# Hybrid decoder layer on one core: gate vectors as running sums, w_in splits moved ahead of the state scan, the attention sink as a 129th key, the gated unit by token tiles

## The chip, the cores and the metric

The kernel runs on one core of one Trainium2 chip. The metric is device time of one launch in microseconds (us), the median over runs. Five engines work side by side, each through its own queue of instructions in order: TensorE (PE, matmuls; its weight loads are listed as PEld), VectorE (DVE), ScalarE (ACT), GpSimd (POOL) and SyncE (SP), which here issues nearly all DMA transfers. Instructions of different engines are tied by semaphores. The order within each queue is fixed when the program is built.

## The reference

One decoder layer over x (1024 tokens by 1024), conditioned on one vector c:

```
mod = silu(c) @ w_ada + b_ada                       # sh1, sc1, g1, sh2, sc2, g2
h = rmsnorm(x, pre_mix_g) * (1 + sc1) + sh1
q, k, v, u = split(h @ w_in)                        # 512, 128, 128, 512 columns
attn = sliding_window_attention(q, k, v, sinks)     # 8 heads, 2 kv heads, window 128, ALiBi,
                                                    # softmax over the keys and one sink logit
ssm = s5_mixer(u, ...)                              # complex diagonal scan per group, then
                                                    # z = gelu(y); z * sigmoid(z @ w_glu + b_glu)
heads = concat(rmsnorm(attn), rmsnorm(ssm))
x = x + g1 * rmsnorm(heads @ w_out, post_mix_g)
h = rmsnorm(x, pre_mlp_g) * (1 + sc2) + sh2
x = x + g2 * rmsnorm(square(relu(h @ w_mlp_in)) @ w_mlp_out, post_mlp_g)
```

## The kernel before

Large products are done as three fp32r matmuls each (`mm3`, lines 85 to 87): high part by high part, high by low, low by high. So every operand is split first: ACT copies the high part, DVE (line 90, the helper `tt`) subtracts it to get the low part.

The order of the work is set by the tile scheduler: it simulates the program as written and gives every engine a fixed queue; tiles with the same tag share memory and so wait for one another (`slot("S3", ...)` is one place in SBUF, and a new tile there waits for the last reader of the old one). Only the PE queue of the MLP is written out by hand. The stages, with their lines and their place in the span:

- 0 to 113 us: loads, norm of x, the part of w_ada for sh1 and sc1, the u projection (`u_step`), and the small tables of the state space model. `mods2` (lines 460 to 480) adds up sh2 and sc2 on DVE as running sums over eight 128-row blocks of w_ada.
- 113 to 140 us: `vp`, the scan's inputs, and DVE's products that form `Vs`.
- 140 to 244 us: the q, k, v projections `pq` (lines 664 to 684), six passes m of 48 matmuls; each loads its columns into `wr`, and splits them into `whi` and `wlo`. Beside them the scan over 8 chunks on DVE (line 608), the tables `Gs` on POOL (lines 627 to 630), the products `kp` of them, their copy `K`, and eight DMAs (line 655) that spread K into the Toeplitz table `T`. `T` lies in the place of `S5`, whose last reader is the sum on K.
- 215 to 290 us: `yp` (lines 704 to 707), the state space output from T, Gs and Vs; gelu gives `z`, transposed and split to `zh`, `zl`.
- 252 to 376 us: attention in 16 units (`scores`, `probs_t`, `values`), with the softmax on DVE and ACT. Between the units lie the gated unit `glu(m, h)` (by blocks of 128 output features) and `gates()`, which computes g1 and g2 on PE in eight steps: 4 DMAs of w_ada into slot S3 (`graw`), 16 matmuls, a sum over partitions, a product with the gain on POOL, and a write to DRAM.
- 365 to 500 us: `po`, heads by w_out, in halves v=1 (ssm) and v=0 (attn); the weights come by `wor` into slots S0, S3, S1, S2 and are split into `woh` (ACT) and `wol` (DVE, two of them POOL). Then residual and second norm.
- 500 to 1202 us: the MLP, in a Strassen-like form, and the last norm.

Of the kernel before, what the change touches and what calls it, by code (L numbers as in the profile page):

```python
# [9 lines left out]
F32 = mybir.dt.float32  # L10
# [23 lines left out]
def tile_hymba(ctx: ExitStack, tc: tile.TileContext, x, c, w_ada, b_ada, pre_mix_g, w_in,  # L34
# [328 lines left out]
    def vecs2():  # L363
        small_loads()
        vps = ps("C", "vps")
        T.transpose(vps[:, 0:20], S5[0:20, 3840:3968], ident[0:20, 0:20])
        V.tensor_copy(vt[:, 64:84], vps[:, 0:20])
        V.tensor_scalar(bgl, bglu, 0.5, None, op0=MUL)
        V.tensor_scalar(nsk, snk, -1.0, None, op0=MUL)

    bgl = ct([P, 4], F32, "bgl")
    nsk = ct([P, 8], F32, "nsk")
# [86 lines left out]

    def mods2():  # L460

        for s in (3, 4):
            acc = slot("S7", [P, D], F32, "macc")
            for q in range(KC):
                ab = slot(("S3", "S6")[q % 2], [P, D], F32, "adm")
                pin(SY.dma_start(ab, w_ada_v[q, :, s * D:(s + 1) * D]))
                if q == 0:
                    pin(V.tensor_scalar(acc, ab, cact[:, 0:1], None, op0=MUL))
                else:
                    pin(V.scalar_tensor_tensor(acc, ab, cact[:, q:q + 1], acc, op0=MUL, op1=ADD))  # L470
                yield
# [10 lines left out]
    gd = {s: dp.tile([P, D], F32, name=f"gate{s}") for s in (2, 5)}  # L482
    w_ada_s = w_ada.rearrange("(q p) (s f) -> p q s f", p=P, s=6)

    def gates():

        gcols = slot("JK", [P, 2, 2 * P], F32, "gcols")
        for s in (2, 5):
            for b in range(4):
                sl = slice(2 * P * b, 2 * P * b + 2 * P)  # L490
                g = gcols[:, b % 2]
                SY.dma_start(g, (post_mix_g if s == 2 else post_mlp_g)[0, sl].partition_broadcast(P))
                srcs = []
                ap_ = ps("C", "ada")
                o = ap_[:, 2 * P:4 * P]
                raw = slot("S3", [P, 4, 2 * P], F32, "graw")
                for q in range(KC):
                    if q % 2 == 0:
                        SY.dma_start(raw[:, q % 4:q % 4 + 2], w_ada_s[:, q:q + 2, s, sl])
                    c0 = 32 * (q % 4)  # L500
                    T.matmul(ap_[c0:c0 + 32, 0:2 * P], cact32[:, q], raw[:, q % 4], start=q < 4, stop=q >= 4)
                part = parts_ada[:, b % 2]
                A.activation(part, ap_[:, 0:2 * P], AF.Copy)
                T.matmul(o, sel, part, start=True, stop=False)
                for e in range(2):
                    r = 64 + 8 * s + 2 * b + e
                    T.matmul(o[:, e * P:(e + 1) * P], ident[64:112, r:r + 1].broadcast_to([48, P]), vrow[64:112],
                             start=False, stop=e == 1)
                A.activation(part, o, AF.Copy)
                tt(PL, g, part, g, MUL)  # L510
                SY.dma_start(gd[s][:, sl], g)
                yield
# [83 lines left out]
    kk_ = ct([P, 2, G], F32, "kk")  # L596
    k1, k2 = kk_[:, 0], kk_[:, 1]
    for C in range(8):
        if C:

            y, x0 = Vs[:, C - 1, :, 15], Vs[:, C, :, 0]
            tt(V, k1, y, Bt[:, 0], MUL)
            tt(V, k2[0:64], y[64:128], Bt[64:128, 1], MUL)
            tt(V, k2[64:128], y[0:64], Bt[0:64, 1], MUL)
            tt(V, x0, x0, k1, ADD)
            tt(V, x0, x0, k2, ADD)
        blk = Vs[:, C].rearrange("p g d -> p (g d)")
        V.tensor_tensor_scan(blk, R, blk, 0.0, op0=MUL, op1=ADD)
# [12 lines left out]
    for qg in range(4):  # L621
# [27 lines left out]
    tt(PL, kd, bc(ident[0:CI, 0:CI], 1, G), bc(dsT, 2, CI), MUL)  # L649
    tt(PL, Kt[:, :, 0:CI], Kt[:, :, 0:CI], kd, ADD)  # L650
# [5 lines left out]

    w_in_q = w_in[:, 0:W].rearrange("(k p) (v i d) -> p k v i d", p=P, v=2, d=64)
    w_in_k = w_in[:, W:W + 256].rearrange("(k p) (m f) -> p k m f", p=P, f=P)  # L660
    qT = slot("B5", [P, 4, 8, P], F32, "qT")
    kT = slot("S4", [P, 8, P], F32, "kT")
    vT = slot("S6", [P, 8, P], F32, "vT")
    for m in [4, 5, 0, 1, 2, 3]:
        wr = slot("S0", [P, KC, P], F32, "wr")
        whi = slot("S1", [P, KC, P], F32R, "whi")
        wlo = slot("S2", [P, KC, P], F32R, "wlo")
        for kk in range(0, KC, 4):
            if m < 4:
                for kv in range(2):  # L670
                    SY.dma_start(wr[:, kk:kk + 4, kv * 64:kv * 64 + 64], w_in_q[:, kk:kk + 4, kv, m, :])
            else:
                SY.dma_start(wr[:, kk:kk + 4, :], w_in_k[:, kk:kk + 4, m - 4, :])
            for k2 in range(kk, kk + 4, 2):
                A.activation(whi[:, k2:k2 + 2], wr[:, k2:k2 + 2], AF.Copy)
                tt(V, wlo[:, k2:k2 + 2], wr[:, k2:k2 + 2], f32(whi[:, k2:k2 + 2]), SUB)
        dst = (qT[:, m] if m < 4 else (kT, vT)[m - 4])
        pq = [ps("A", "pq") for _ in range(2)]
        for k in range(KC):
            for h in range(2):  # L680
                mm3(pq[h], whi[:, k, :], wlo[:, k, :], hh[h][:, k, :], hl[h][:, k, :], k == 0, k == KC - 1)
        for h in range(2):
            o = dst.rearrange("p n (j l) -> p j n l", j=8)[:, 4 * h:4 * h + 4]
            A.activation(o, pq[h].rearrange("p (j n l) -> p j n l", j=4, n=8), AF.Copy)
# [45 lines left out]
    SB = AB[:, 0:2].rearrange("p a (u i k) -> p (a u) i k", u=2, i=4)  # L730
    Vd = AB[:, 2].rearrange("p (n d) -> p n d", n=8)
    PB = slot("B1", [P, 4, 1024], F32, "PB")
    rf = AB[:, 2, 0:256].rearrange("p (h q) -> p h q", h=2)
    tmp = AB[:, 2, 256:512].rearrange("p (h q) -> p h q", h=2)
    dtab = AB[:, 2, 512:768].rearrange("p (h q) -> p h q", h=2)
    tb16 = AB[:, 3].bitcast(BF16)
    before = AB[:, 3, 640:768]
# [5 lines left out]
    for i in range(8):  # L743
        V.tensor_scalar(slI[:, i], ident, -8.0 * SLOPES[i], None, op0=MUL)
# [26 lines left out]
    def scores(u, hook=None):  # L771
# [3 lines left out]
        st_ = ct([P, 3, 4], F32, f"sm{u % 4}")  # L775
        nmx, den, es = st_[:, 0], st_[:, 1], st_[:, 2]
# [3 lines left out]
        for i in range(2):  # L780
            for t in range(2):
                for kv in range(2):
# [687 lines left out]
```

## Time and profile before

| | |
|---|---|
| runs | median 1210.9 us (1210.22 to 1212.89, 3 runs) |
| profiled execution | 1204.21 us, span of its instructions 1202.4 us |
| busy over the span | PE 1083.2 us (90%), DVE 906.4 (75%), ACT 566.6 (47%), POOL 551.3 (46%) |
| chain that ended last | PE 40%, DVE 11%, ACT 3% |
| DMA | 96.08 MB, mean 80 GB/s |

The profiled execution is 6.7 us faster than the median of the other runs. PE is the busiest engine in every long stage, so the question for each stage is when PE stands still, and what it does while it works. A wait is listed under the instruction that waited, with the work that ended it after an arrow.

### The profile page before, as it was taken

The numbers are of one execution on the slowest core, as the hardware profiler recorded it, in microseconds if no ns is written. First come the engines' busy times: TensorE is split into PE (matmuls) and PEld (weight loads), VectorE is DVE, ScalarE is ACT, GpSimd is POOL, SyncE is SP. The second block draws the span as 40 slices with busy tenths as digits, with TensorE's granted clock in tenths as the row PEclk, the third lists the DMA queues.
The fourth block names the chain that finished last, engine by engine and source line by source line (L and its number), as shares of the span: only waits on it lengthen the run. The fifth ranks groups of instructions, "written<-read, shape, count | busy, mean of one in ns | idle before, by whom it ended". The sixth has DMA issues, their size and how long they took to land.

```text
span 1202.4 us, 15127 instructions
## 1 busy us (share of the span) xinstructions
PE 1083.2 (90%) x5263; PEld 840.4 (70%) x5263; DVE 906.4 (75%) x1478; ACT 566.6 (47%) x1221; POOL 551.3 (46%) x477
## 2 busy tenths in 40 slices
PE   5889949899997899889999999999999999999796
PEld 3667737775553688768778777877877787787685
DVE  3596781159881155697999989999998999998956
ACT  4552014356663155557554455455445545444431
POOL 5951242012664144452455455455545545554735
PEclk9998979999997799989999999999999999999898
DMA  9935014301256223302101201210120121012135
GB/s 274 254 112 182 5 27 55 65 27 36 87 162 164 79 88 105 123 26 71 53 27 62 71 27 44 71 53 27 62 71 27 45 70 53 27 62 70 35 106 193
DMA packets 96573, 96.08 MB, mean 80 GB/s; under 512 B 22256, under 2 KB 77920, under 8 KB 96480
## 3 DMA queue, kind: packets, MB, share of 16 engines
q1 hardware_dynamic: 96160, 95.08, 26.8%
q8 instruction: 41, 0.67, 0.2%
q14 instruction: 36, 0.29, 0.1%
q10 hardware_dynamic: 240, 0.02, 0.0%
q0 software_dynamic: 96, 0.02, 0.0%
HBM read 84.48 MB, written 9.44 MB: 78 GB/s over the span
## 4 chain that ended last, share of the span: by engine, by line
PE 40%; DVE 11%; ACT 3%; issue 2%; DMA 1%; POOL 0%; POOLq 0%; DVEq 0%; ACTq 0%; SPq 0%
PE fo L85 7%; PE fi L87 7%; PE fi L85 7%; PE fi L86 7%; PE fo L86 7%; PE fo L87 7%; DVE facc L90 4%; DVE f L90 3%; DVE w L90 2%; DVE xo L1396 1%; ACT ops L1086 1%; ACT tmpc L1320 1%; ACT h2s L1086 0%; DVE ops L90 0%; DVE h2s L90 0%
## 5 line engine op out<-in xcount | busy, mean ns | idle before, releaser
L90 POOL TENSOR_TENSOR facc<-facc,tmpc 128x512 f32<-128x512 f32 x106 | 153.7, 1450 | 203.7 <-ACT tmpc L1320 188.8
L90 DVE TENSOR_TENSOR facc<-facc,fo 128x512 f32<-128x512 f32 x335 | 221.1, 673 | 13.7 <-PE fo L87 13.5
L85 PE MATMUL fo<-ops 128*128 128x512 f32 x264 | 105.2, 398 | 16.0 <-DVE facc L90 16.0
L86 PE MATMUL fo<-ops 128*128 128x512 f32 x264 | 103.3, 391 | 0.0
L87 PE MATMUL fo<-ops 128*128 128x512 f32 x264 | 103.3, 391 | 0.0
L87 PE MATMUL fi<-h,w 128*128 128x512 f32 x248 | 97.4, 393 | 5.7 <-DVE w L90 5.7
L85 PE MATMUL fi<-h,w 128*128 128x512 f32 x248 | 97.2, 392 | 0.0
L86 PE MATMUL fi<-h,w 128*128 128x512 f32 x248 | 97.0, 391 | 0.0
L90 DVE TENSOR_TENSOR w<-w1r,w 128x256 fp32r<-128x256 f32 x169 | 91.5, 550 | 4.1 <-ACT w L1086 3.6
L1086 ACT ACTIVATE ops<-f 128x512 fp32r<-128x512 f32 x66 | 41.5, 628 | 105.3 <-PE fo L86 99.4
L1165 ACT ACTIVATE f<-f 128x512 f32<-128x512 f32 x60 | 37.9, 632 | 102.5 <-DVE f L90 102.3
L1086 ACT ACTIVATE w<-w1r 128x256 fp32r<-128x256 f32 x169 | 68.7, 409 | 33.9 <-PE fi L86 24.7
L90 DVE TENSOR_TENSOR f<-fi,f 128x512 f32<-128x512 f32 x120 | 80.3, 680 | 3.9 <-PE fi L87 3.7
L90 DVE TENSOR_TENSOR ops<-f,ops 128x512 fp32r<-128x512 f32 x66 | 60.2, 912 | 25.4 <-ACT ops L1086 15.6
L90 POOL TENSOR_TENSOR w2r<-w2r,w2r 128x512 f32<-128x512 f32 x35 | 48.1, 1376 | 56.2 <-DMA w2r<-in_w_mlp_out_dram 20.6
L85 PEld LDWEIGHTS fo<-ops 128*128 128x128 f32 x264 | 49.9, 189 | 33.5 <-DVE facc L90 23.4
L90 POOL TENSOR_TENSOR w1r<-w1r 128x256 f32<-128x256 f32 x60 | 66.3, 1114 | 11.0 <-DVE w L90 9.6
L1320 ACT ACTIVATE tmpc<-fo 128x512 f32<-128x512 f32 x106 | 61.7, 582 | 11.0 <-POOL facc L90 8.8
L85 PE MATMUL fo<-h2s 128*128 128x512 f32 x128 | 50.9, 397 | 9.0 <-DVE facc L90 9.0
L87 PEld LDWEIGHTS fi<-h,w 128*128 128x128 f32 x248 | 46.9, 189 | 15.9 <-DVE w L90 6.1
L87 PEld LDWEIGHTS fo<-ops 128*128 128x128 f32 x264 | 49.8, 189 | 10.5
L86 PEld LDWEIGHTS fo<-ops 128*128 128x128 f32 x264 | 49.9, 189 | 9.5
(376 smaller groups left out, 2985.2 us busy)
## 6 DMA issues: line engine op xcount, KB each, us to landing
w2r<-in_w_mlp_out_dram SPq DMA_DIRECT2D x64, 256.0 KB, 2.8
ad<-in_w_ada_dram SPq DMA_DIRECT2D x32, 256.0 KB, 5.7
adm<-in_w_ada_dram SPq DMA_DIRECT2D x16, 512.0 KB, 3.6
w1r<-in_w_mlp_in_dram SPq DMA_DIRECT2D x32, 256.0 KB, 3.4
graw<-in_w_ada_dram SPq DMA_DIRECT2D x32, 256.0 KB, 3.1
w1r<-in_w_mlp_in_dram SPq DMA_DIRECT2D x16, 512.0 KB, 3.9
xn<-in_x_dram SPq DMA_DIRECT2D x8, 512.0 KB, 5.9
xin<-in_x_dram SPq DMA_DIRECT2D x8, 512.0 KB
```

Source lines behind the costliest of these rows:

```text
L85: T.matmul(ps, lh, rh, start=first, stop=False)
L86: T.matmul(ps, lh, rl, start=False, stop=False)
L87: T.matmul(ps, ll, rh, start=False, stop=last)
L90: e.tensor_tensor(o, a, b, op=op)
L1086: A.activation(hi, src, AF.Copy)
L1165: A.activation(o, o, AF.Relu)
L1320: A.activation(tmpc, p_, AF.Copy)
L1396: V.scalar_tensor_tensor(xin[:, sl], ag_[:, j % 4, sl], r_, xin[:, sl], op0=MUL, op1=ADD)
```

## The change

1. `gates()` no longer uses PE for the products: it adds up eight blocks of w_ada on DVE, as `mods2` does (new helper `ada_acc`), adds b_ada to one row, and one matmul with a matrix of ones sums over the partitions and spreads the result to all of them. Gate 5 goes to DRAM, gate 2 stays in SBUF. Its steps stand in the loop over m of the projections. `mods2` has three load slots in place of two.
2. The projections' code stands ahead of the scan and the tables; `wr` is split in two halves of four blocks each, one ACT and one DVE instruction per half, in two slots (S1, S2). The query scale is folded into the copy out of PSUM.
3. Tables Gs and the sum on K go from POOL to DVE.
4. The sink logit is column 129 of each score row, so the softmax's maximum and sum take it in; six small DVE and ACT instructions per unit go, one ACT copy per unit comes.
5. `glu(j)` works by 128-token tiles: z is stationary, w_glu moves; the bias comes by two matmuls from one row; the sum of squares comes from an ACT instruction; four transposes per tile bring the result back to features by tokens. POOL has no part in it.
6. All low parts of w_out are made on DVE.

```
+    def ada_acc(s, acc, raws):
+        for q in range(KC):
+            ab = slot(raws[q % len(raws)], [P, D], F32, "adm")
+            pin(SY.dma_start(ab, w_ada_v[q, :, s * D:(s + 1) * D]))
+            if q == 0:
+                V.tensor_scalar(acc, ab, cact[:, 0:1], None, op0=MUL)
+            else:
+                V.scalar_tensor_tensor(acc, ab, cact[:, q:q + 1], acc, op0=MUL, op1=ADD)
+            yield
...
     def gates():
-        ... 16 matmuls per step on w_ada, 8 steps, slot S3
+        for s, gain in ((5, post_mlp_g), (2, post_mix_g)):
+            acc = slot("G1S", [P, D], F32, "macc")
+            yield from ada_acc(s, acc, ("S3", "S7"))
+            brow = slot("S3", [1, D], F32, "brow")
+            pin(SY.dma_start(brow, b_ada[:, s * D:(s + 1) * D]))
+            tt(V, acc[0:1], acc[0:1], brow, ADD)
+            gb = slot("S7", [P, D], F32, "gb")
+            pin(SY.dma_start(gb, gain[0].partition_broadcast(P)))
+            yield
+            g = acc if s == 2 else gb
+            for h in range(2):
+                gp = ps("D", "gp")
+                sl = slice(h * 512, h * 512 + 512)
+                T.matmul(gp, ones, acc[:, sl], start=True, stop=True)
+                tt(V, g[:, sl], gp, gb[:, sl], MUL)
+            if s == 5:
+                SY.dma_start(gd5, g)
+            else:
+                g1[0] = g
+            yield
...
+    for m in [4, 5, 0, 1, 2, 3]:          # now ahead of the scan and the tables
+        wr = slot("S0", [P, KC, P], F32, "wr")
+        for kh in range(2):
...
+            w_ = slot(("S1", "S2")[kh], [P, 2, 4, P], F32R, "wqk")
+            A.activation(w_[:, 0], wr[:, k4], AF.Copy)
+            tt(V, w_[:, 1], wr[:, k4], f32(w_[:, 0]), SUB)
...
+        bg_steps(4)
+    bg_steps(99)
...
-        tt(PL, Gs[:, gs, 1:8], bc(cst[:, 0, gs], 2, 7), pwr, MUL)
-        tt(PL, tg, bc(cst[:, 1, gs], 2, 7), pwi, MUL)
-        tt(PL, Gs[:, gs, 1:8], Gs[:, gs, 1:8], tg, ADD)
+        tt(V, ...)                        # the same three, and the two on K
...
+        V.tensor_reduce(nmx, Sb, axis=AX.X, op=ALU.max, negate=True)     # 129 wide
         for i in range(4):
-            A.activation(Sb[:, i], sc[i], AF.Exp, scale=0.125, bias=nmx[:, i:i + 1], accum_out=den[:, i:i + 1])
-        A.activation(es, es, AF.Exp)
-        tt(V, den, den, es, ADD)
+            A.activation(Sb[:, i], Sb[:, i], AF.Exp, bias=nmx[:, i:i + 1], accum_out=den[:, i:i + 1])
...
+    def glu(j):
+        for k in range(4):
+            mm3(gp, zh[:, k, sl], zl[:, k, sl], wgh[k // 2][:, k % 2], wgl[k // 2][:, k % 2], k == 0, False)
+        for e in range(2):
+            T.matmul(gp, ones_r, bgr[:, e], start=False, stop=e == 1)
+        A.activation(th, gp, AF.Tanh, scale=0.5)
+        V.scalar_tensor_tensor(sg, th, 1.0, z[:, j], op0=ADD, op1=MUL)
+        A.activation(th, sg, AF.Square, scale=0.5 / 32.0, accum_out=ssz[:, j:j + 1])
+        for f in range(4):
+            T.transpose(tp[:, f * P:(f + 1) * P], sg[:, f * P:(f + 1) * P], ident)
+        A.activation(hi, tv, AF.Copy, scale=0.5)
+        V.scalar_tensor_tensor(lo, tv, 0.5, f32(hi), op0=MUL, op1=SUB)
...
     def wout_lo(v, i):
-        if (v, i) in [(1, 1), (1, 3)]:    # two on POOL
```

What the scheduler makes of it shows in three places of the queues.

First, DVE within the scan (line 608 before, 682 now; each chunk begins with a SCALAR_TENSOR_TENSOR on R and Vs, and its small products, kk before and m2 now, follow). In the kernel before, the first split of the second pass (wlo, of m=5) comes after the sixth scan chunk:

```order
L608 SCALAR_TENSOR_TENSOR Vs_130_1035<-R_129_1004,Vs_130_1035 128x512
L90 TENSOR_TENSOR wlo_167_1375<-wr_165_1373,whi_166_1374 128x256
L90 TENSOR_TENSOR kk_148_1177<-Vs_130_1035,par_23_129 128x32
L90 TENSOR_TENSOR kk_148_1177<-Vs_130_1035,par_23_129 64x32 x2
L90 TENSOR_TENSOR wlo_167_1375<-wr_165_1373,whi_166_1374 128x256 x2
```

In the changed kernel the split of m=5 (wqk) comes after the second chunk, and the tables on Gs and s5 stand in the same queue:

```order
L682 SCALAR_TENSOR_TENSOR Vs_128_1030<-R_127_999,Vs_128_1030 128x512
L90 TENSOR_TENSOR wqk_160_1251<-wr_159_1249,wqk_160_1251 128x512
L90 TENSOR_TENSOR m2_129_1031<-Vs_128_1030,par_23_129 128x32
L90 TENSOR_TENSOR m2_129_1031<-Vs_128_1030,par_23_129 64x32 x2
L90 TENSOR_TENSOR Vs_128_1030<-Vs_128_1030,m2_129_1031 128x32 x2
L682 SCALAR_TENSOR_TENSOR Vs_128_1030<-R_127_999,Vs_128_1030 128x512
L630 TENSOR_SCALAR s5_28_152<-cps_205_1622,sgn_13_99 128x512
```

The splits moved ahead of most of the scan, and the scan now shares DVE with the tables.

Second, PE at the end of the projections. In the kernel before, the last eight of the 32 products kp stand inside the third pass (m=0, whose products are pq_173 and pq_174, with the low part wlo_172); the first yp stands behind the fourth pass (m=1), with two passes still to come after it:

```order
L85 MATMUL pq_174_1454<-h1h_36_160,whi_171_1439 128x512
L86 MATMUL pq_174_1454<-h1l_38_162,whi_171_1439 128x512
L639 MATMUL kp_153_1268<-Gs_150_1229,s5_28_152 16x128 x8
L87 MATMUL pq_174_1454<-h1h_36_160,wlo_172_1440 128x512
L85 MATMUL pq_173_1453<-h1h_35_159,whi_171_1439 128x512
```

In the changed kernel 26 of the 32 kp stand behind the last projection (pq_204 is the last pass), and behind them the scores of five units before the first yp:

```order
L87 MATMUL pq_204_1571<-h1h_34_158,wqk_202_1567 128x512
L653 MATMUL kp_208_1648<-Gs_206_1630,s5_28_152 16x128 x10
L653 MATMUL kp_209_1669<-Gs_206_1630,s5_28_152 16x128 x2
L499 MATMUL gp_199_1556<-macc_177_1397,ones_12_97 128x512
L653 MATMUL kp_209_1669<-Gs_206_1630,s5_28_152 16x128 x14
L659 MATMUL dps_210_1690<-ident_2_68,dsk_5_78 16x32
L759 MATMUL vt_242_1978<-ident_2_68,vT_148_1174 128x128 x4
```

What moved is the whole chain from kp to T: it now begins where the projections end.

Third, SP around the write of gate 5. Before, the gates' loads (graw) and the writes of their results alternate, and the last load of w_out's ssm half (wor_315) stands behind them:

```order
L511 DMA gate5_673<-gcols_247_2120 128x256
L499 DMA graw_300_2669<-in_w_ada_dram 128x2x256 x2
L912 DMA wor_315_2783<-in_w_out_dram 128x1024
L511 DMA gate5_673<-gcols_247_2120 128x256
L1016 DMA g1p_347_2989<-gate2_672 128x1024
```

In the changed kernel the write of gate 5 stands among the projections' loads, and the second running sum's loads (adm_178 on) behind it:

```order
L604 DMA wr_189_1479<-in_w_in_dram 128x4x64 x2
L502 DMA gate5_668<-gb_174_1388 128x1024
L460 DMA adm_178_1398<-in_w_ada_dram 128x1024
L604 DMA wr_189_1479<-in_w_in_dram 128x4x64 x2
L862 DMA th_250_1997<-in_b_glu_dram 1x512
L460 DMA adm_179_1401<-in_w_ada_dram 128x1024
```

The gates' loads left the stage ahead of po, and w_out's eight loads no longer share S3 with them.

More of the change, by code (lines that the diff above doesn't have):

```diff
@@ L458, in tile_hymba @@
     w_ada_v = w_ada.rearrange("(k p) n -> k p n", p=P)
+    def ada_acc(s, acc, raws):
[7 more added lines that the diff above has]
+            yield
     def mods2():
         for s in (3, 4):
[L463 to L471, printed above, removed]
+            acc = slot("G1S", [P, D], F32, "macc")
+            yield from ada_acc(s, acc, ("S3", "S6", "S7"))
             mp = ps("D", "mp")
@@ L480, in mods2 @@
             yield
-    gd = {s: dp.tile([P, D], F32, name=f"gate{s}") for s in (2, 5)}
-    w_ada_s = w_ada.rearrange("(q p) (s f) -> p q s f", p=P, s=6)
+    gd5 = dp.tile([P, D], F32, name="gate5")
+    g1 = {}
     def gates():
[L487 to L512, printed above, removed]
@@ L655, in tile_hymba @@
         SY.dma_start(Tt[CI * s:CI * s + CI, :, CI * j:P], Kt[:, :, 0:P - CI * j])
[L659 to L684, printed above, removed]
+    k1, k2 = m2[:, 0, 0:G], m2[:, 0, G:2 * G]
+    for C in range(8):
+        if C:
+            y, x0 = Vs[:, C - 1, :, 15], Vs[:, C, :, 0]
+            tt(V, k1, y, Bt[:, 0], MUL)
+            tt(V, k2[0:64], y[64:128], Bt[64:128, 1], MUL)
+            tt(V, k2[64:128], y[0:64], Bt[0:64, 1], MUL)
+            tt(V, x0, x0, k1, ADD)
+            tt(V, x0, x0, k2, ADD)
+        blk = Vs[:, C].rearrange("p g d -> p (g d)")
+        V.tensor_tensor_scan(blk, R, blk, 0.0, op0=MUL, op1=ADD)
     z = slot("B8", [P, 8, W], F32, "z")
@@ L872, in glu @@
-    def glu(m, h):
-        whi, wlo = glw[m]
+    w_glu_k = w_glu.rearrange("(k p) f -> p k f", p=P)
+    wgh = [slot(("S0", "S1")[i], [P, 2, W], F32R, "wgh") for i in range(2)]
+    wgl = [slot(("S2", "S6")[i], [P, 2, W], F32R, "wgl") for i in range(2)]
+    th = slot("JK", [P, W], F32, "th")
+    ssz = ct([P, NT], F32, "ssz")
+    ones_r = slot("PW", [1, P], F32R, "ones_r")
+    V.tensor_copy(ones_r, ones[0:1])
+    wgr = [slot(t, [P, 2, W], F32, "wgr") for t in ("G2S", "S3")]
+    for i in range(2):
+        SY.dma_start(wgr[i], w_glu_k[:, 2 * i:2 * i + 2, :])
+        A.activation(wgh[i], wgr[i], AF.Copy)
+        tt(V, wgl[i], wgr[i], f32(wgh[i]), SUB)
@@ L927, in wol0 @@
             pin(wout_lo(0, i))
+    for u in range(4):
+        sink(u)
     scores(0)
@@ L931, in tile_hymba @@
     scores(2)
-    bg = gates()
     for n in range(8):
-        if n < 4:
-            glu_w(n)
         if n == 6:
```

165 lines of the change are left out of this document (76 added, 89 removed).

## The prediction

> **What bounds the kernel now.** I read the page first: which engine is full, and where it is not.
>
> ```profile
> PE   5889949899997899889999999999999999999796
> PEclk9998979999997799989999999999999999999898
> ```
>
> These are 40 slices of 30 us. PE is full in nearly all of them; it dips in the sixth (150 to 180 us) and the thirteenth (361 to 391 us), and there the granted clock dips too. From the 17th slice on (the MLP) the change moves nothing, so I look only at 113 to 412 us; by 412 us both kernels have to have done the same work, the first 48 products of w_out. Next I read PE's busy time in that stretch, the share of the gates in it (tile ada, two windows), and the windows with a low clock:
>
> ```profile
> 140.00:412.00 272.00, 230.72 (x1316) 157.37 (x1317) 148.34 (x293) 119.28 (x314) 101.22 (x76) 0.89 0.30 77
> ...
> 280.00:365.00 85.00, 13.26 (x104) 5.40 (x104) 0.00 (x0) 3.40 (x9) 0.98 0.38 112
> 365.00:412.00 47.00, 16.68 (x72) 6.65 (x72) 0.00 (x0) 2.68 (x7) 0.71 0.46 134
> ```
>
> ```profile
> 157.00:175.00 18.00, 6.32 (x30) 4.53 (x31) 16.48 (x42) 0.00 (x0) 1.77 (x1) 0.53 0.13 29
> 215.00:219.00 4.00, 3.97 (x22) 4.00 (x23) 1.52 (x4) 2.65 (x6) 0.00 (x0) 0.60 0.26 57
> 268.00:277.00 9.00, 6.96 (x28) 2.97 (x28) 6.79 (x17) 6.08 (x22) 1.72 (x1) 0.62 0.01 2
> 358.00:362.00 4.00, 3.58 (x16) 1.76 (x16) 3.41 (x5) 2.72 (x7) 2.90 (x3) 0.57 1.07 341
> 378.00:406.00 28.00, 17.34 (x61) 9.31 (x61) 0.93 (x3) 4.44 (x8) 8.21 (x5) 0.51 0.40 120
> ```
>
> The columns are the window, its length, PE busy, weight loads, then the other engines in order (in the first row DVE, ACT, POOL), and near the end the granted clock. So of 272 us PE works 230.7 and stands still 41.3. Work at clock c loses the share 1 - c: 6.32 x 0.47 + 3.97 x 0.40 + 6.96 x 0.38 + 3.58 x 0.43 + 17.34 x 0.49 = 17.2 us. At full clock PE's work there is 213.5 us. What ends the idle time stands in PE's waits (us in total, times, longest):
>
> ```profile
> PE pq L87 <- DVE wlo L90: 15.7, 1, 15.7
> PE ada L501 <- DMA graw<-in_w_ada_dram: 8.8, 7, 3.3
> PE yp L704 <- DMA wr<-in_w_in_dram: 5.3, 1, 5.3
> PE sc L784 <- ACT AB L816: 2.9, 1, 2.9
> ...
> PE po L1005 <- ACT woh L915: 1.9, 1, 1.9
> ```
>
> The first is one split that stands in DVE's queue behind six scan chunks; the second is the gates' loads; the third is named wr, but that transfer follows T's on the same queue, so it is T that is late.
>
> **1. Splits ahead of the scan; tables on DVE.** How long DVE takes beside POOL and alone:
>
> ```profile
> 142.37 2.54 DVE L608 TENSOR_TENSOR_SCAN Vs<-R,Vs 128x512 f32<-128x512 f32 x1
> 144.94 5.12 DVE L90 TENSOR_TENSOR kk<-Vs,par 128x32 f32<-128x32 f32 x3
> ...
> 161.04 0.65 DVE L90 TENSOR_TENSOR kk<-Vs,par 128x32 f32<-128x32 f32 x3
> 161.72 0.46 DVE L90 TENSOR_TENSOR Vs<-Vs,kk 128x32 f32<-128x32 f32 x2
> 162.22 1.22 DVE L608 TENSOR_TENSOR_SCAN Vs<-R,Vs 128x512 f32<-128x512 f32 x1
> ```
>
> ```profile
> L470 DVE SCALAR_TENSOR_TENSOR macc<-adm,cact,macc 128x1024 f32<-128x1024 f32 x8 | 10.7, 1342 | 7.3 <-DMA adm<-in_w_ada_dram 7.3
> ...
> L90 DVE TENSOR_TENSOR Vs<-Vs,m 128x512 f32<-128x512 f32 x8 | 5.5, 685 | 0.1
> ...
> L87 PE MATMUL pq<-h1h,wlo 128*128 128x512 f32 x96 | 37.9, 405 | 15.7 <-DVE wlo L90 15.7
> ```
>
> While POOL computes Gs (before 156 us), a chunk of the scan takes 2.54 + 5.12 + 3.9 us; alone it takes 1.22 + 0.65 + 0.46 = 2.33. With POOL empty all eight take 18.6 us. DVE then has, from 141 us: scan 18.6, ten splits of 512 columns at 0.69 (the 128x512 row) 6.9, twelve table products of 896 columns at 0.685 x 896/512 = 1.2, 14.4, the second running sum 10.7, and some 11 of small products (gate products, bias rows, the mask): 62 us. PE's cover is six passes of 48 pq; they start 0.23 us apart where they run freely (tile pq, below, has 288 in 70.6 us of busy time). So DVE is inside its cover by some 8 us, and the split of m=5, now behind two chunks (5 us) under a first pass of 11 us, is on time: the 15.7 us go. I leave 4 us for passes whose split or load comes late, bounds 0 and 10, from the same list of waits.
>
> The first running sum falls into the scan's inputs (113 to 140 us), where DVE is busy 18.9 of 27 us in the trace: 10.7 us into 8.1, most of it earlier than 140. I take 1.5 us, bounds 0 and 2.6.
>
> **2. T now begins where the projections end.** The chain as it ran before:
>
> ```profile
> 189.42 0.63 PE L639 MATMUL kp<-Gs,s 128*16 128x128 f32 x16
> 190.12 2.39 ACT L642 ACTIVATE K<-kp 16x512 f32<-16x512 f32 x4 [4.78 <-PE kp L639]
> 192.59 1.29 POOL L90 TENSOR_TENSOR K<-K,s 16x512 f32<-16x512 f32 x1 [6.18 <-ACT K L642]
> 193.92 3.63 ACT L652 ACTIVATE T<-ident 128x4096 f32<-128x4096 f32 x1 [1.40 <-POOL K L90]
> ...
> 197.57 10.59 SPq L655 DMA_DIRECT2D T<-K  x8
> ...
> 215.03 0.77 PE L704 MATMUL yp<-T,U 128*128 128x128 f32 x2 [5.33 <-DMA wr<-in_w_in_dram]
> ```
>
> Before, kp's last part stood in the third pass, and pq covered most of this. Now 26 kp stand behind the last pq. From there: 26 kp at 0.63/16 us, 1.0; ACT's four K copies 2.4, two of Gw 1.2 (0.6 each, as K's), four more of K 2.4, two of Gw and two of scores 2.4 (the sum on K runs under them), T's zeros 3.6; and 17.5 from T's first transfer to the first yp (197.57 to 215.03). That is 30.5 us. What PE has in it:
>
> ```profile
> 140.00:412.00 272.00, 35.91 (x192) 11.03 (x128) 20.12 (x32) 3.01 (x16) 0.89 0.30 77
> ...
> 140.00:412.00 272.00, 70.62 (x288) 54.92 (x288) 7.08 (x12) 0.89 0.30 77
> ...
> L504 PE MATMUL ada<-adc 128*128 128x256 f32 x16 | 6.2, 476 | 1.5 <-ACT adc L503 1.5
> ...
> L716 PE MATMUL zt<-ident,z 128*128 128x128 f32 x32 | 4.9, 279 | 0.0
> ```
>
> The rows are tile sc, tile pq, and two groups. A unit of scores is 35.91/16 = 2.24 us, five are 11.2; eight vt and eight pt at zt's 0.15 are 2.4; kp 1.0; one gate product 1.2 (below). Together 15.8, so PE waits 14 to 15 us for T; I take 14.5. Bounds: 4 (only the 17.5 us and the zeros count) and 22 (two units of scores wait for the mask, which stands behind the second sum on DVE). This is the late step in place of the split.
>
> **3. Gates off PE, sink, gated unit.** The gates took 22.4 us at full clock (13.26 us for 104 of 176 records). Added: four gate products. L504 is eight instructions of 256 columns in 6.2 us, part of it at half clock; twice the columns would be 1.55 each, at full clock some 1.2, so 4.7 in all (bounds 4.4 and 6.2). Sixteen bias matmuls at pq's 0.25: 4.0. Sixteen groups of transposes, as many instructions as zt: 4.9.
>
> ```profile
> 280.00:412.00 132.00, 4.10 (x32) 3.95 (x32) 0.33 (x2) 0.88 0.41 120
> ...
> 286.00:365.00 79.00, 76.48 (x468) 43.77 (x464) 67.59 (x132) 49.16 (x153) 50.17 (x46) 0.98 0.41 121
> ...
> adm<-in_w_ada_dram SPq DMA_DIRECT2D x16, 512.0 KB, 3.6
> ```
>
> Half of rp (first row) goes with the sum of squares on ACT: 2.0. The second row is attention: PE 76.5 and DVE 67.6 of 79. Without the gates PE has 63 left there, fewer than DVE's 67.6; the six small instructions of each unit that go, and POOL's products beside DVE that go, lower DVE's; the two low parts of w_glu and the gated unit's products stay. So DVE comes near to PE. Idle of PE in attention: 0 if DVE falls as far as PE, 12 if DVE sets the pace and the gated units stand where they do; I take 6.
>
> **4. w_out.** The eight loads wait for slots that the last gated unit frees, with no gates left to run beside them.
>
> ```profile
> 396.10 0.34 SPq L912 DMA_DIRECT2D wor<-in_w_out_dram  x1
> ...
> 400.77 0.79 PE L1005 MATMUL po<-woh,hd 128*128 128x512 f32 x1 [1.85 <-ACT woh L915]
> ```
>
> A load, its high part and the first product took 4.7 us in a row. I take 5 us of idle PE (bounds 2 and 9, the second if the loads go one by one). The low parts on DVE find it idle: no cost; if that cover were gone, the products with the low part would come late next. The wait for gate 2 is gone with its trip to DRAM.
>
> **The clock.** A wait of 2.9 us ahead of 270 us was followed by a low clock until 276; its loss is 2.6 us, and after longer waits 3 (157 to 175). For T's wait and w_out's I take 3.5 each, 7 us, a little above these rows since w_out's loads leave PE short of work for longer than one wait. The Trainium skill, "TensorE: Matmul & The Clock Gate", Part 1, says that the array falls to half clock after a window of about 3.4 us without work and is back after about 3.4 us of steady work. By that rule two waits would lose 1.7 us each, 3.4 in all, an estimate from its figure, and the time would be 3.6 us lower. The trace agrees that the clock halves and returns, but here a wait shorter than its window was enough, and the low stretch was twice as long.
>
> **The sum, 140 to 412 us.** PE's work 213.5 - 22.4 - 2.0 + 4.7 + 4.0 + 4.9 = 202.7. Low clock 7. Idle 4 (passes) + 14.5 (T) + 6 (attention) + 5 (w_out) = 29.5, where 41.3 stood. With 1.5 ahead of 140 us: 240.7 instead of 272, that is 31 us less. The profiled execution took 1204.21 us (span 1202.4), and the median of the runs is 6.7 us above it; 31 us off the median gives 1180 us.
>
> **Rivals.**
> - Dearer waits: scores do not fill T's wait (the mask comes late: 22 instead of 14.5) and DVE sets attention's pace (12 instead of 6), with passes late by 10 instead of 4: 19.5 us worse, gain 11.5, 1199. For it: DVE has only 8 us of slack in the projections. Against: the trace's DVE is slow there only beside POOL.
> - T is covered better: the wait is 4, and attention runs without idle: 16.5 better, gain 47.5, 1163; halfway, 1171. For it: a quiet queue, since the 17.5 us shared it with a wr load. Against: T's eight issues alone take SP 10.6.
> - The split's wait stays: if another split stands late by as much (15.7 instead of 4), 12 worse, gain 19, 1192. Against: its place in DVE's queue.
> - Slower: the running sums' loads run one after another. A step is then 3.6 for the load, 0.33 for its issue (as at 396.10) and 1.34 for the product, 5.3 us, instead of half of that, 2.65, with two slots. Sixteen steps would add 42 us, and splits and K's sum stand behind them on DVE: 11 us slower, 1222. It decides from 31/16 = 1.9 us more per step, a step of 4.6 us. Against: the same kind of sum in the trace waited 7.3 us in eight steps, 0.9 each.
>
> **How the numbers follow.** A difference under 0.2% (2.4 us) is about what a measurement can't tell from none. The forecast (gain 22 to 42, 1169 to 1189) has 0.55, dearer waits 0.20, better cover 0.15, the split's wait 0.03, slower 0.05; 0.02 is left for no change, where several of these costs just cancel the gain. Faster is 0.55 + 0.20 + 0.15 + 0.03 = 0.93, same 0.02, slower 0.05. The range 1165 to 1200 leaves out slower, no change, the part of dearer waits beyond their sum (0.06) and the part of better cover beyond halfway (0.06): 0.19.
>
> **What would show it.** Right: no wait of pq for a split over 3 us; a wait of yp of 10 to 18 us soon after the last pq, near 225 to 242 us, and a clock near 0.5 behind it; no ada on PE; a wait of po of 3 to 7 us; DVE's scan chunks at 2.3 us each. Wrong: waits of pq for low parts whose own wait is on adm; waits of scores or pv for DVE of more than 10 us in all.

## The result, and the profile after

Beside the kernel before on one chip (four runs each), the changed kernel took a median of 1173.5 us, from 1155.9 to 1175.5, against 1210.9 us. The ratio, which leaves out two of the four runs as slow, is 0.961, with a 95% interval of 0.949 to 0.973. In a second comparison, six runs with 17 of the kernel before, the median was 1155.9 us (1152.4 to 1173.8) against 1211.4 and the ratio 0.954 (0.950 to 0.959). The change is faster by 47 us by the first ratio and 55 by the second; the forecast was 31, and 0.961 of 1210.9 is 1163.7, just below its range of 1165 to 1200. The intervals are wide because the changed kernel's runs stand at two levels, 1152 to 1157 us with a mean granted clock of 0.974 to 0.978, and 1172 to 1176 with 0.952 to 0.959. The traces shown of it are of the lower level: the profiled execution took 1155.87 us, 48.3 less than the profiled execution of the kernel before.

The page's rows for PE and its clock, again 40 slices, of 29 us here:

```profile
PE   4889999789998998799999999999999999999795
PEclk9999999989998999899999999999999999999898
```

The dip to 4 at 150 to 180 us is gone; what is left are a dip to 7 around the eighth slice (202 to 231 us) and one in the seventeenth (462 to 490 us), where the MLP begins. PE's four longest waits ahead of 400 us:

```profile
PE yp L702 <- DMA T<-K: 5.3, 1, 5.3
PE po L1000 <- ACT mix L1005: 3.2, 1, 3.2
PE pt L818 <- DVE AB L90: 2.3, 1, 2.3
PE pq L85 <- ACT wqk L608: 1.7, 1, 1.7
```

No low part and no load of w_ada is among them. These windows are read as before (window, length, PE, PEld, DVE, ACT, POOL, clock): the first pq to the 48th product of w_out, which took 272 us before; the last pq to the first yp; and from there to the end of attention.

```profile
136.50:359.70 223.20, 207.50 (x1183) 149.82 (x1181) 150.90 (x264) 120.89 (x305) 15.63 (x20) 0.96 0.26 69
209.50:237.00 27.50, 15.10 (x131) 8.32 (x132) 18.84 (x43) 23.57 (x70) 2.08 (x1) 0.83 0.32 44
237.00:343.00 106.00, 105.78 (x672) 73.59 (x672) 68.17 (x121) 72.37 (x197) 9.55 (x16) 0.98 0.06 21
```

PE works 207.5 us in the first window and stands still 15.7; 4.8 us of its work are loss to a low clock, worked out as in the prediction over the stretches at half clock, so 202.7 us are work at full clock. The second window holds nearly all of the idle time, 12.4 us; 5.3 of them are yp's own wait for T, and 7.1 are waits of the scores (sc), the transposes (pt, vt) and their like for DVE and ACT. In the third PE stands still 0.2 us of 106. T's chain, whose first row is the last group of kp:

```profile
211.26 1.05 PE L653 MATMUL kp<-Gs,s 128*16 128x128 f32 x28
...
214.01 2.39 ACT L656 ACTIVATE K<-kp 16x512 f32<-16x512 f32 x4
...
216.43 1.69 DVE L90 TENSOR_TENSOR K<-K,s 16x512 f32<-16x512 f32 x1 [1.08 <-ACT K L656]
...
218.26 3.62 ACT L666 ACTIVATE T<-ident 128x4096 f32<-128x4096 f32 x1
...
221.91 8.69 SPq L669 DMA_DIRECT2D T<-K  x8
...
237.02 0.77 PE L702 MATMUL yp<-T,U 128*128 128x128 f32 x2 [5.30 <-DMA T<-K]
```

It ends 27.5 us behind the last pq, where the prediction had 30.5; 15.1 of them are from T's first transfer to the first yp, where the trace of before had 17.5.

### The profile page after: what moved, and what is told of

The parts are those of the page before. It is cut to its first block, busy times and chain, and to the rows that moved or that the text cites. A ratio compares the mean times of both kernels' runs of the same rounds, so it can differ in the third digit from the quotient of the medians.

```text
span 1154.1 us, 14738 instructions
## 1 busy us (share of the span) xinstructions
PE 1056.8 (92%) x5127; PEld 830.5 (72%) x5127; DVE 914.1 (79%) x1452; ACT 570.0 (49%) x1213; POOL 470.1 (41%) x421
## 4 chain that ended last, share of the span: by engine, by line
PE 62%; DVE 19%; DMA 7%; ACT 5%; issue 4%; POOL 2%; SPq 1%; DVEq 0%; POOLq 0%; ACTq 0%
PE fi L87 7%; PE fo L85 7%; PE fi L85 7%; PE fi L86 7%; PE fo L86 7%; PE fo L87 7%; DVE facc L90 4%; DVE f L90 3%; DVE w L90 2%; PE po L1000 2%; PE po L1001 2%; PE po L1003 2%; DMA adm<-in_w_ada_dram 2%; PE vp L579 1%; DVE macc L464 1%
## 5 line engine op out<-in xcount | busy, mean ns | idle before, releaser
L90 DVE TENSOR_TENSOR ops<-f,ops 128x512 fp32r<-128x512 f32 x66 | 60.5, 917 | 25.2 <-ACT ops L1080 15.1
```

The costliest lines, as they stand in the source:

```text
L90: e.tensor_tensor(o, a, b, op=op)
```

## The experiments

Each kernel is compared with the kernel before, and with the changed kernel by its level and its trace. e1 to e4 share one chip, and so do e5 to e8, e9 to e12, and the last two; the four chips differ, and each group has runs of the kernel before on its own chip (medians 1209.6 to 1211.5 us).

### e1 to e3: the same kernel again, and two parts alone

e1 is the changed kernel, unaltered.

> The changed kernel, unaltered. Its runs stand at two levels so far, one at 1156 us with a mean granted clock of 0.974 and three at 1172 to 1176 with 0.952 to 0.958. Theory A: the same waits of PE are followed now by shorter, now by longer stretches at half clock; a profile at the upper level would show PE's idle time before 365 us within 3 us of the 19.7 us of the first profile and about 17 us more loss by a low clock, wherever it lies. Theory B: a transfer or a wait is longer in those runs; then PE's idle time is 10 us or more above the first profile's in one named wait.

Six runs: 1152.4, 1152.7, 1155.2, 1156.6 (the profiled one), 1171.7, 1173.8, so four at the lower level and two at the upper. The profile is of the lower one, so it answers neither theory; idle time, low clock and waits agree with the first trace to 1 us. The levels were left to e4 to e9.

e2, the gates alone:

```
 kernel before
+    bg = gates()                  # the new one, ada_acc with slots S3 and S7
     for m in [4, 5, 0, 1, 2, 3]:
...
+        bg_steps(4)
...
-            glu(n, 0); bg_steps(1); glu(n, 1); bg_steps(1)
+            glu(n, 0); glu(n, 1)
```

> The kernel before with the gates alone as running sums in the projections' loop; all else as before. Theory A (the sum of the prediction): PE loses 22.4 us of gates and gains 4.7 of gate products, the low clock around 378 to 406 us loses 8.5 and w_out's wait keeps about 3 of it, the gates' 8.8 us of load waits and 2 of copies go and 5 for w_out come: about 29 us faster, 1182. The split's 15.7 us wait stays. Rival: the running sums delay DVE's splits and T's chain in the projections by what they save later; less than 12 us faster, over 1198.

Median 1188.8 (1181.0 to 1192.6), ratio 0.982 (0.977 to 0.986): 22 us faster, between the two, and 7 short of theory A. PE's longest waits in this kernel:

```profile
PE pq L87 <- DVE wlo L90: 11.2, 1, 11.2
PE gp L511 <- DVE gb L90: 8.1, 1, 8.1
PE pq L85 <- ACT whi L681: 7.0, 3, 4.3
```

The split's wait stays, and two more come, which I read as a DVE queue that now holds the running sums beside POOL's tables. That is the place the rival named, at less than half of its size. This trace also has half clock from 131.0 to 148.1 us, in vp and the first pq, which costs 8.5 us and which the trace of the kernel before does not have there. The shortfall is not the clock's, though: the two runs clear of the others, 1181.0 and 1182.7, against the six fastest of the kernel before, 1203.0 to 1205.5, give the same 22 us.

e3, the order alone:

```
 kernel before
-    scan, tables + kp + T, projections
+    projections, tables + kp + T, scan
```

> The kernel before with the code of the projections ahead of the scan and the tables, and nothing else. Theory A: the wait of 15.7 us for the split goes with 1 to 3 us of low clock, and T stays covered by four passes: 15 to 19 us faster, 1192 to 1196. Rival: the scan now ends late, beside POOL's tables, and yp waits for it or for T: under 8 us faster.

Median 1208.0, ratio 0.999 (0.995 to 1.002): no difference. The row answering to the 15.7 us:

```profile
PE pq L87 <- DVE wlo L90: 18.1, 3, 14.9
```

The wait isn't gone; it has moved to a later pass. Theory A falls: the code's order alone buys nothing. What holds the split up is in e5.

### e5 and e6: what took the split's wait away

e5:

```
 changed kernel, Gs (3 lines) and the two products on K
-        tt(V, ...)
+        tt(PL, ...)
```

> The changed kernel with the tables Gs and the two products on K back on POOL. Theory A (the prediction's): the split was late because DVE ran beside POOL; with POOL at work again scan chunks take 5 to 11 us, pq waits 8 to 15 us for a low part, and the kernel is 8 to 16 us slower than the changed one at the same level (1164 to 1172 at the lower). Theory B: the wait went because the split is made in two halves in two slots, each free at half a pass; then pq's waits for low parts stay under 3 us and the time within 5 us of the changed kernel.

Six runs, two at 1172.5 and 1173.2, four at 1191 to 1195: 17 to 19 us slower than the changed kernel at either level. PE's first wait, and DVE beside POOL ahead of it:

```profile
PE pq L87 <- DVE wqk L90: 17.1, 1, 17.1
```

```profile
160.70 3.80 DVE L90 TENSOR_TENSOR m<-Vs,par 128x32 f32<-128x32 f32 x3
162.62 1.84 POOL L90 TENSOR_TENSOR s<-s,pw 128x896 f32<-128x896 f32 x1
164.54 2.13 POOL L90 TENSOR_TENSOR Gs<-Gs,s 128x896 f32<-128x896 f32 x1
164.54 2.20 DVE L90 TENSOR_TENSOR Vs<-Vs,m 128x32 f32<-128x32 f32 x2
166.74 1.78 POOL L90 TENSOR_TENSOR s<-s,pw 128x896 f32<-128x896 f32 x1
166.77 2.83 DVE L682 TENSOR_TENSOR_SCAN Vs<-R,Vs 128x512 f32<-128x512 f32 x1
```

Here small DVE products of 32 columns last until a POOL product of 896 has ended: the three at 160.7 take 3.80 us, in the changed kernel 0.65. They end at 164.50, just behind POOL's at 164.46, and the two at 164.54 end at 166.74, just behind POOL's at 166.67, so DVE waits whole POOL instructions out. Theory A holds, and is larger than expected (8 to 16): the tables on DVE, with order and splits unchanged here, are worth 17 to 19 us. That this is also the length of the wait is chance. From the first pq to the 48th product of w_out this kernel takes 242.1 us, 18.9 more than the changed kernel, made up of 9.5 us more of idle PE (25.2, since T's wait is 1.1 here) and 9.0 us more lost to half clock (13.8). The Trainium skill, "SBUF — State Buffer", "SBUF: two separate sides", says that VectorE and GpSimd hold a shared pair of ports for a whole instruction, and that the second to come blocks, if VectorE's operation has two inputs in SBUF and GpSimd's reads SBUF. The trace agrees in the ends just given.

e6:

```
 changed kernel
-            w_ = slot(("S1", "S2")[kh], [P, 2, 4, P], F32R, "wqk")   # half a pass, high and low
+        whi, wlo = slot("S1", ...), slot("S2", ...)                  # a whole pass, 256 columns at a time
```

> The changed kernel with the splits as before: the high parts of a whole pass in S1, the low parts in S2, 256 columns at a time; the tables stay on DVE. Theory B: a pass's split can start only where the pass before ends, and pq waits 8 us or more in all for high and low parts between passes. Theory A: with POOL empty the splits are on time, waits under 3 us in all. The last kp stand two passes earlier in PE's queue here, so T's wait of 13 us goes in both: by B the time is within 6 us of the changed kernel's, by A 10 to 16 us faster.

All six runs 1169.4 to 1176.4. In the trace vp ran at half clock (below); from the first pq to the 48th product of w_out it takes 222.5 us, the changed kernel 223.1. The waits for low parts:

```profile
PE pq L87 <- DVE wlo L90: 5.2, 2, 4.2
```

5.2 us is between the two theories: by this one trace the halves in two slots are worth some 5 us of waits, beside e5's 17. T's wait went here, as expected, and other waits came (yp for z, for a gate product and for Gw, 5.8 us in all), so idle PE is 15.3 us, where the changed kernel has 15.7.

### e4, e7, e10 to e12: taking T's wait away

e4 and e7, the code of the tables moved:

```
 changed kernel
-    passes 4, 5, 0, 1, 2, 3; tables, kp, T; scan
+    passes 4, 5; tables, kp, T; passes 0, 1, 2, 3; scan        # e4
+    passes 4, 5, 0, 1, 2; tables, kp, T; pass 3; scan          # e7
```

> The changed kernel with the code of the tables, kp and T between the second and the third pass of the projections, so that three passes lie between the last kp and the first yp. Theory A: the 13 us in which PE stood idle between the last projection and the first yp go, and with them most of 13.7 us at half clock: 13 to 18 us faster than the changed kernel in the same state, 1138 to 1143 at its lower level and 1156 to 1160 at its upper. Rival: the tables stand in DVE's queue ahead of splits, and passes wait for splits instead: within 5 us of the changed kernel, or slower.

> The changed kernel with the code of the tables, kp and T ahead of the last pass of the projections, one and a half passes of pq then lie between the last kp and the first yp. Theory A: the 13 us of idle PE ahead of the first yp fall to 0 to 4, and the low clock behind them to 2 to 4: 10 to 15 us faster than the changed kernel at the same level, 1139 to 1146 at the lower. Rival: as with the tables between the second and third pass, other waits (splits, gate products behind the running sum, first yp for its products on DVE) take their place: within 4 us or slower.

e4: 1180.0 (1165.3 to 1181.9), e7: 1167.0 (1151.8 to 1170.5). Waits of e4, then of e7:

```profile
PE gp L499 <- DVE macc L90: 9.5, 2, 8.7
PE pq L85 <- ACT wqk L609: 4.3, 1, 4.3
...
PE yp L703 <- DMA T<-K: 1.7, 1, 1.7
```

```profile
PE yp L703 <- DMA T<-K: 9.0, 1, 9.0
PE sc L785 <- DVE AB L753: 2.8, 1, 2.8
```

In e4 T's wait falls to 1.7 us, as theory A has it, and the rival's waits take its place: the second running sum is pushed back on DVE, and the gate product that needs it stops PE for 8.7 us. In e7 kp ends 13 us ahead of the last pq, but the sum on K stands behind the running sum on DVE and runs only at 223.7; T's wait is longer than in the changed kernel. e4 is slower at both levels. e7 gains little: its one run at the lower level, 1151.8, stands beside the changed kernel's lowest, 1152.4, and its five upper runs, 1166.1 to 1170.5, lie a few us below that kernel's 1171.7 to 1175.5, as does the stretch from the first pq to the 48th product of w_out in its trace (219.2 us, 3.9 less). The forecast was 10 to 15.

e10 holds the diagonal of K in R's place, so that T's zeros wait for the last kp and not for the sum on K; e11 also issues every second transfer of T from ACT; e12 also has the code of the tables ahead of the last pass. All three start from e8 (below).

```
-    kd = S5[0:CI, 1536:2048]...
+    kd = R[0:CI, 0:512]...                                 # e10, e11, e12; scan ahead of it
-        SY.dma_start(Tt[...], Kt[...])
+        (SY, A)[s % 2].dma_start(Tt[...], Kt[...])         # e11, e12
```

> The changed kernel with pq dealt out between the groups of vp, and the diagonal term of K held in R instead of in S5, so that T's zeros wait for the last kp and no longer for the sum on K. With vp mixed alone the zeros began at 213.0 us, 5.0 behind the last kp at 208.0, the first yp at 231.8. Theory A (T's chain sets the first yp): the zeros begin 2 to 3 us sooner, and the kernel takes 1145 to 1148. Rival: ACT's queue holds the zeros to the same place, no change from 1147 to 1151.

> As the kernel before it in this list, and the eight transfers of T issued in turn by SP and ACT in place of SP alone, where their issue takes 8.8 us. Theory A: the last transfer is issued 4 us sooner, the first yp comes 3 to 4 us sooner: 1141 to 1145. Rival: the landing and not the issue sets the end, or ACT's issues hold up the softmax of the first units: no gain, or 1 to 3 us slower.

> As the one before, with the code of the tables, kp and T ahead of the last pass of the projections. Theory A: the first kp leave the end, some 10 to 15 us of T's chain lie beside the last pass, the wait of yp for T is under 1 us: 1136 to 1143. Rival: the last pass's split, the gate products or K's sum come later on DVE by as much; within 3 us of the one before it.

e10: zeros at 210.8 instead of 213.0, the first yp at 229.5 instead of 231.8, as expected; the time is 1149.1 (1147.3 to 1150.3) and e8's 1149.6 (1147.6 to 1151.4), so the 2.3 us can't be told in the time. e11: 1154.4 (1154.0 to 1154.9), 5 us slower. Its trace:

```profile
217.24 3.69 SPq L695 DMA_DIRECT2D T<-K  x4
...
220.04 3.36 ACTq L695 DMA_DIRECT2D T<-K  x1
223.45 1.26 ACT L812 ACTIVATE AB<-sc 128x256 f32<-128x256 f32 x4 [3.66 <-issue]
...
223.88 0.70 PE L796 MATMUL sc<-AB 128*128 128x256 bf16 x2 [4.00 <-ACT AB L812]
```

SP's half is issued in 3.7 us, but ACT's last one ends at 223.4, and ACT copies scores only then, for which PE waits 4.0 us: the rival. e12 runs in 1149.4 (1146.7 to 1152.5): T's wait is gone from the list, but scores wait for ACT (3.8 us) and for the mask (2.8), and PE's idle time from the first pq to the 48th product is 10.4 us, in e10 10.8. T's wait is the last of several that end within a few us of one another; taking one away shows the next.

### e8 and e9: the two levels

The stretch of vp just ahead of the projections, 112 to 136 us, in the changed kernel, and the same window in e4, e6 and e7 in turn, each from its own trace:

```profile
112.00:136.00 24.00, 24.00 (x188) 15.45 (x188) 19.77 (x27) 0.60 (x1) 0.00 (x0) 1.00 0.45 135
```

```profile
112.00:136.00 24.00, 24.00 (x108) 15.02 (x110) 11.03 (x16) 0.60 (x1) 0.00 (x0) 0.50 0.33 103
```

```profile
112.00:136.00 24.00, 24.00 (x110) 15.65 (x110) 12.21 (x16) 0.60 (x1) 0.00 (x0) 0.50 0.40 119
```

```profile
112.00:136.00 24.00, 24.00 (x106) 14.28 (x104) 12.72 (x18) 0.60 (x1) 0.00 (x0) 0.50 0.36 110
```

PE is never idle in any of them, and does 188 matmuls in one and 106 to 110 in the others: the granted clock is 1.00 there and 0.50 here. In e4 the half clock begins at 108.9 us and lasts 47.8 us, to the first pq, although PE works all the time; half of that, 24 us, is lost, and the difference of the levels is 17 to 20. A run's record points the same way without a trace. The clock is 0.50 or 1.00 in every trace here, so a run has spent twice the missing share of its mean clock at 0.50: 51 to 60 us in the changed kernel's lower runs (2 x 0.026 x 1154 is 60) and 96 to 113 in its five upper ones, 36 to 62 us more. So e8 deals the first pass of pq out between vp's groups:

```
 changed kernel
     for qg in range(8):
         vp, vs = ...            # 12 products of 128 columns
+        pass_step(st4, qg)      # one eighth of pass m=4: six products of 512 columns
```

The edit also moves vp's tiles to other places in PSUM (the rotation AABABAC becomes ABABC); that alone was not tried.

> The changed kernel with the first pass of pq dealt out between the eight groups of vp, six pq behind each group. Theory C (the two levels of 1153 to 1157 and 1172 to 1176 come from the stretch of vp, which stays at half clock to its end if it starts so): pq between the groups lifts the clock within a group or two, all runs stand within 8 us of one another, at 1148 to 1160. Theory D (the levels come from waits elsewhere): a third to a half of the runs still stand some 17 us above the rest.

Six runs, 1147.6 to 1151.4, median 1149.6; ratio 0.949 (0.945 to 0.952). The upper level is gone, and the 22 runs of e10 to e13, which have the same edit, do not show it either (1146.7 to 1154.9). e6 and e7, on the same chip as e8, had 11 of 12 runs at the upper level. Its own window, PE at 1.00:

```profile
112.00:136.00 24.00, 24.00 (x178) 17.65 (x176) 19.27 (x27) 1.23 (x2) 0.00 (x0) 1.00 0.43 132
```

This is theory C, shown by the runs; that the changed kernel's upper runs are vp at half clock stays an inference, since none of them left a trace. The same window in e12, and then in e9 (the kernel before with the same edit), shows what the edit does:

```profile
112.00:136.00 24.00, 24.00 (x170) 17.42 (x170) 17.92 (x24) 1.23 (x2) 0.00 (x0) 0.93 0.43 132
```

```profile
112.00:136.00 24.00, 24.00 (x168) 18.34 (x165) 14.27 (x19) 3.31 (x7) 0.00 (x0) 0.88 0.27 86
```

The clock still falls, but it comes back: the half clock lasts 3.4 us in e12 (from 112.8 us) and 6.8 in e9 (from 130.3), where it lasted 34 to 51 in e4, e6, e7 and e14. PE stood still 2.0 us ahead of vp in e12, as it did in e4. e9 itself, the kernel before with that edit:

> The kernel before with its first pass of pq dealt out between the groups of vp, six pq behind each; nothing else changed. Theory C (the upper runs of the kernel before, 1209 to 1218 us at clocks of 0.943 to 0.956, have vp at half clock as well): the runs gather at 1194 to 1205, with no run above 1207. Theory D (its spread comes from the waits behind vp): runs still reach 1209 to 1218.

Twelve runs, 1201.5 to 1208.8 (one above 1207, eleven to 1205.3), beside 17 of the kernel before from 1203.3 to 1213.8; ratio 0.996 (0.994 to 0.997). The spread shrinks and the median comes down 5.7 us, which fits theory C in the main. It is not shown for the kernel before: no upper run of it left a trace, and its 17 runs here lie within 11 us, less than the 24 that half clock through all of vp cost in e4. With pq between vp in both, the medians are 1203.9 and 1149.6, 54 us apart (on two chips): that is the change with little left of vp's clock. e8, e10 and e12 are the fastest versions here, ahead of both kernels.

### The last two: attention, and the stretch ahead of the projections

```
 e8, in glu(j), behind the square
+        for _ in range(4):
+            PL.tensor_tensor(scr, z[64:128, j], z[64:128, j], op=MUL)   # nobody reads scr
```

> The changed kernel with pq dealt out between the groups of vp (1147.5 to 1151.4 us, one level), and four products of 512 columns on POOL, whose result nobody reads, behind the square of each gated-unit tile: 32 in all, about 40 us of POOL work in attention, near what the kernel before had there. Theory A (attention lost its waits since POOL is quiet beside DVE): DVE's instructions beside them take two to three times as long, PE's idle time between the last yp and the first po rises from under 1 us to 4 to 10, the time is 1153 to 1160. Rival (DVE has slack enough in the new attention, the small sink instructions that went made the room): PE's idle time there stays under 2 us, 1148 to 1152.

1150.2 (1148.1 to 1151.4): no difference from e8. Groups of this kernel between 262 and 342 us, POOL's added work and two of DVE's:

```profile
L894 POOL TENSOR_TENSOR bgr<-z 64x512 fp32r<-64x512 f32 x32 | 36.4, 1137 | 4.4 <-DVE wgl L90 2.0
...
L810 DVE TENSOR_REDUCE AB<-sc 128x256 f32<-128x512 f32 x20 | 12.9, 679 | 0.5 <-PE sc L799 0.5
L90 DVE TENSOR_TENSOR AB<-AB,sm 128x512 f32<-128x512 f32 x11 | 10.2, 929 | 0.2
```

The product with two inputs in SBUF took 709 ns in e8 and takes 929 here; the reduction that reads PSUM took 684 and takes 679. PE stands still 0.7 us of 79, as in e8 (0.8). The rival holds: a quiet POOL is not why attention has no waits; DVE has room. Its work behind the last yp (262 us before, 267 now) and up to po fell, by these windows of the kernel before and of the changed one:

```profile
267.00:365.00 98.00, 92.60 (x558) 51.79 (x555) 84.25 (x173) 63.89 (x209) 52.68 (x48) 0.95 0.33 97
```

```profile
267.00:343.00 76.00, 75.79 (x456) 47.13 (x454) 56.02 (x101) 54.37 (x165) 9.55 (x16) 1.00 0.06 21
```

DVE does 84.3 us in the first and 56.0 in the second: 28 us less, where PE does 17 less. The groups of the first window show two sources. One is the small instructions on the sink logit, three of each unit on DVE, which are gone:

```profile
L90 DVE TENSOR_TENSOR sm<-sm,snk 128x4 f32<-128x4 f32 x15 | 7.2, 478 | 0.2
...
L90 DVE TENSOR_TENSOR sm<-sm 128x4 f32<-128x4 f32 x15 | 6.4, 426 | 7.5 <-ACT sm L817 7.5
...
L811 DVE SCALAR_TENSOR_TENSOR sm<-sm,nsk 128x4 f32<-128x4 f32 x15 | 4.4, 296 | 0.1
...
L819 DVE RECIPROCAL sm<-sm 128x4 f32<-128x4 f32 x15 | 2.5, 170 | 0.2
```

```profile
L806 DVE RECIPROCAL sm<-sm 128x4 f32<-128x4 f32 x10 | 1.7, 171 | 6.1 <-ACT AB L805 6.1
```

They are 18.0 us. The other source is the place of the work: the last row of each fence is one reciprocal per unit, so 15 of the 16 units have their softmax in the first window and 10 in the second. The changed kernel does the other six ahead of 267 us, five of them before the first yp at 237.0, in the stretch where PE waits for T. The four groups of the softmax fall by 12 us in the window for that reason (reductions, products and reciprocals, 40.9 to 28.5). So T's wait pays for a part of the quiet attention. What either source is worth alone was not tried.

```
 changed kernel, mods2
-            yield from ada_acc(s, acc, ("S3", "S6", "S7"))
+            yield from ada_acc(s, acc, ("S3", "S6"))
```

> The changed kernel with two load slots in place of three for the running sums of sh2 and sc2. Theory A (the third slot is what brings the first pq forward, from 140.3 to 136.5 us): the first pq starts at 138 to 140, 1 to 3 us slower at the same level. Rival: the first pq stays within 0.8 us of 136.5 at the same low clock ahead of it, and the time within 1 us.

Five runs, 1169.0 to 1172.6. vp fell to half clock at 119.6 us in its trace, so the times don't answer. With the low clock taken out (17.2 us lost here, 6.4 in the changed kernel), the stretch from 10 us to the first pq takes 123.1 us, and 119.9 in the changed kernel: 3.2 us longer. That speaks for theory A. Worked out the same way, the six traces with three slots and vp unmixed (the changed kernel, e1, e4 to e7) give 118.6 to 122.7 us and the four with two (the kernel before, e2, e3, e14) 123.1 to 126.5: the direction is borne out, the size is not sure. All five runs stand about where the changed kernel's upper level is, and five of that kernel's ten do; so the third slot, or the chip, may also bear on how vp is entered, which was not tried.

## Why the prediction was right or wrong

**Work of PE.** Forecast 202.7 us at full clock, measured 202.7 (202.8 in e1). The total came out as the rows of before had it; the single terms agree less well (the gate products take 4.2 us where 4.7 stood, the transposes 4.9 as forecast), so that it is exact is luck.

**The low clock.** Forecast 7 us for T's wait and w_out's, measured 6.5 (4.8 to the 48th product, 1.7 behind it). The half clock around T's wait lasted from 227.5 to 241.1 us, longer than I had it, but PE was idle for more than half of that time.

**Idle time: the step that failed.** Forecast 29.5 us, measured 18.9 (15.7, and 3.2 behind the 48th product). By its terms: attention 6 forecast, 0.2 measured; passes 4 and 1.7; T 14.5 and 12.4; w_out 5 and 4.2, and 0.4 elsewhere. T's wait and w_out's stand where the prediction put them, and each term was sized too large. In T's place it had one wait of yp of 10 to 18 us behind filled time; yp waits 5.3, and the rest is scores and transposes that wait for their softmax. Attention is the worst: the prediction compared PE's 63 us with DVE's 67.6 and named the six sink instructions that go, but did not add up their rows (18 us on DVE), did not see that six units' softmax would be done ahead of the last yp, and took POOL's quiet for half of the reason. e13 shows that it is not; how much each of the other two did stays open.

**The stretch ahead of 140 us: the second term that failed.** For the first running sum 1.5 us more were forecast; the stretch came out 3.6 us shorter (126.3 us from the transposes at 10 us to the first pq, where it was 129.9). With the low clock taken out of both it is 119.9 and 126.5, 6.6 us shorter. The sum itself costs PE nothing to be seen there (DVE has it under vp). That the third slot for the sums of sh2 and sc2 could bring the stretch forward was not in the prediction; e14 gives it 3.2 us, and the rest is open, since the traces of one form differ by 3 to 4 us among themselves.

Together: 10.6 us less idle time, 5.1 in the stretch ahead and 0.5 of clock make 16.2 us beyond the 31.3 forecast, 47.5 in all, and the two profiled executions are 48.3 apart.

**The split.** Its wait went, as forecast, and for the reason given (POOL beside DVE), as e5 shows. That the order of the code does it, as the same part has it ("the split of m=5, now behind two chunks ... is on time"), is not so: e3 has that order and a wait of 14.9 us in a later pass.

**The sum against the median.** The prediction took its 31 us off a median that was 6.7 us above the profiled execution, as if that gap were noise. e9, whose median is 5.7 us lower, suggests that it is in good part vp's clock; in the changed kernel the two levels are 17 to 20 us apart. This was in no term and no rival, and which levels the runs of a comparison happen to stand at is luck: the two ratios, 0.961 and 0.954, differ by it. Of the rivals, slower, dearer waits and a split that stays did not come about. Better cover of T, forecast at 1163 to 1171, has the right time, and half of its reason: attention runs without idle time, but the 12.4 us at T stay.

## What to carry to other kernels

Before costing a table or an elementwise step on POOL, look at what DVE does beside it: two-input DVE instructions can then last as long as POOL's (three small products 3.80 us in place of 0.65 in e5; less in e13, 929 ns in place of 709), and whoever waits for DVE pays it. Sum an engine's rows in the stage before and after instead of guessing whether it comes near the bound, and ask whether part of its work has moved to another stage. And when runs of one kernel stand at two levels, read the granted clock window by window: a long stretch of small matmuls may run at half clock from end to end, and here a few wide matmuls dealt into it settled the matter.

## What the runs showed of the hardware

Half clock can last through 44 to 51 us of matmuls without a gap (e4 47.8, e6 51.2, e7 44.4 us), when they are mostly vp's float32 products of 128 columns, two in three of them with weights 64 wide; it ended within 3 us of the first pq, 512 columns wide. The Trainium skill, "TensorE: Matmul & The Clock Gate", Part 1, has the clock back after about 3.4 us of steady work; the trace does not agree for this kind of work. With six such pq behind every twelve of vp it lasted 3.4 us (e11, e12, e13) and 6.8 us (e9) where it came at all. What starts it stays open: PE had stood still for 2.0 and 2.2 us a few us earlier in e4 and e6, for 0.7 and 0.2 in e7, and about as long as in e7 in the changed kernel's own trace, which stayed at full clock in vp; in e2 it began at 131.0 and in e9 at 130.3, in the midst of vp, with no wait.
